# The last block of each MLP's down projection as seven quarter products

## The chip, the cores and the metric

The kernel runs on one core of one Trainium2 chip. The metric is the device time of one execution in microseconds. The kernel before takes 1024.99 us, the median of three runs (1024.59 to 1025.01). Five engines work side by side, each with its own queue: TensorE (PE in the profile; PEld are its weight loads), VectorE (DVE), ScalarE (ACT), GpSimd (POOL) and SyncE (SP), which issues most transfers. POOL issues the accumulating transfers, which add what they load to what stands in the tile.

## The reference

A trunk of two layers over 512 tokens of width 1024, all in float32. Each layer is a mixer, a layer norm, an MLP and a layer norm:

```python
def _layernorm(x, g, b):
    mu = xf.mean(-1, keepdims=True)
    var = jnp.square(xf - mu).mean(-1, keepdims=True)
    return ((xf - mu) * lax.rsqrt(var + LN_EPS) * g + b).astype(x.dtype)

def _mlp(x, w_up, w_down):          # w_up 1024 x 4096, w_down 4096 x 1024
    h = jax.nn.relu(x @ w_up)
    return (h * h) @ w_down

    for l in range(DEPTH):          # DEPTH = 2, alpha = sqrt(2)
        y = _mla(...) if l < n_a else _swa(...)
        x = _layernorm(alpha * x + y, ln_mix_g[l], ln_mix_b[l])
        x = _layernorm(alpha * x + _mlp(x, mlp_w_up[l], mlp_w_down[l]), ln_mlp_g[l], ln_mlp_b[l])
    return x
```

Layer 0 has latent attention (`_mla`), layer 1 sliding-window attention (`_swa`). The change touches the two calls of `_mlp` and the norm behind each.

## The kernel before

**Numbers in two parts.** Every matrix product takes its operands as a high part, rounded by ScalarE, and a low part, the rest, which is a subtraction on VectorE. `split` (L71 to L82) makes the two: ScalarE at L76, the low part at L79, on VectorE unless the caller names GpSimd. `three` (L107) turns one product into three matmuls: high by high, high by low, low by high.

**Blocks and sevens.** The hidden width of 4096 is cut into four blocks q of 1024. `up` of a block gives 1024 hidden values for 512 tokens, `down` multiplies them with the block's 1024 rows of `w_down` and adds to the residual stream `xs`, four row tiles of 128 tokens by 1024. Up of every block and down of blocks 0 to 2 are products of 2 x 2 quarters, made by a seven-product scheme. One quarter product of `down` covers 256 tokens (two row tiles t), 512 columns and a depth of 512 (four chunks m): 2 x 4 x 3 = 24 matmuls with 512 columns each. It takes a factor (a sum of hidden quarters, in the tile `fac`, three buffers) and a sum of weight quarters.

**Weights.** The sums of weight quarters are grown in place. `queue_seven` (L164) loads a quarter in two halves jp of 512 KB, splits it into `wh` and `wl` (four buffers each), and then lets POOL issue an accumulating transfer of the next quarter onto it (L188). So products 1, 5, 6 and 4 hang on one chain (tile `quada`), 3 and 7 on another (`quadb`), and 2 loads alone. Each link is a split, an accumulating transfer, and the next split. The function `weights` hands out the pairs in order and prepares at most four tiles ahead (`AHEAD`); a tile made "aside", in a spare place, doesn't count in that ring.

**Order.** PE and SP work strictly in the order of the program (`pe`, L92). On the other engines a planner orders what is ready by its own costs, with the order of the program as priority; `tc.high_priority()` puts a part ahead, and `pinned` keeps its vector instructions in order. The steps of an MLP are written out in `STEPS`, `FIRST_STEPS` and `LAST_STEPS` (L39, L40): U'5 is product 5 of up of block q + 1, D5 product 5 of down of block q. A factor is made two steps ahead of its product.

**The last block.** Down of block 3 is plain: `TokMajor` (L425) takes four row tiles, two halves of 512 columns and eight chunks, 192 matmuls, with eight plain weight tiles of 512 KB. Its `finish` (L451) first makes the left half of all row tiles, chunk pair by chunk pair, then the right half row tile by row tile. After each row tile come its add and statistics (`add_last`, L538; `count`, L520) and its norm (`layer_norm`, L387): aggregate, a root on POOL (`rsqrt_of`, L375), and two passes over the row tile on VectorE. In layer 0 the finished row tiles are turned for the next stage (`turn_tokens`, L404): eight transposes on PE, in its order, and a split. In layer 1 they go out.

**Before the last block**, the running sum `u2` of products 1 and 6 of blocks 0 to 2 is brought into `xs` by six vector instructions after D6 of block 2 (L778 to L782).

Of the kernel before, what the change touches and what calls it, by code (L numbers as in the profile page):

```python
# [15 lines left out]
P = 128  # L16
D = 1024
# [22 lines left out]
FIRST_STEPS, LAST_STEPS = "U'1 U'2 U'5 U'3 U'6 U'7 U'4 D'1 D'2", "U'1 D5 U'2 D3 U'5 D6 D7 U'3 U'6 U'7 U'4 D4"  # L40
# [8 lines left out]
def build(tc, nc, io, out):  # L49
    with ExitStack() as top:  # L50
# [113 lines left out]
        def queue_seven(name, key, chunk):  # L164
# [18 lines left out]
            def grown(a, jp, *more, aside=None):  # L183
                wh, wl = tiles_of_weights(aside)
                with behind(state.pop("first", None) if (key, a, jp) == ("U", "b", 1) else None):
                    split(wh, wl, flat(half(a, jp)), keep=(a, bool(more)) == ("b", True) and key == "U")
                if more:
                    nc.gpsimd.dma_start(half(a, jp), chunk(*more, jp), accum_op=ALU.add)  # L188
                return wh, wl
# [5 lines left out]
            def alone(jp, aside=None):  # L195
# [10 lines left out]
                4: lambda jp: grown("a", jp),  # L206
# [37 lines left out]
        def mlp_stream(l):  # L244
# [392 lines left out]
        def mlp(src, gb, dst, mp):  # L637
# [17 lines left out]
            class Block:  # L655
# [68 lines left out]
                def factor(self, n, quad=False):  # L724
                    if quad:
                        f = mp.tile([P, 2, 4, 256], F32R, tag="quada", bufs=1, name=nm("fac"))
                    else:
                        f = mp.tile([P, 2, 4, 256], F32R, tag="fac", bufs=3, name=nm("fac"))
                    g = [self.g.get(a) for a in ("a11", "a12", "a21", "a22")]
                    split(f[:, 0], f[:, 1], g[2] if n == 0 else self.down.sum(n, *g))  # L730
                    self.fac[n] = f

                def down_(self, n):
                    w = [weights("down") for _ in range(2)]
# [32 lines left out]
            for i, (which, q, n) in enumerate(steps):  # L767
                if which == "D":

                    i_q = steps.index(("U", q, {1: 6, 2: 2}.get(n, 4)))  # L770
                    i_last = steps.index(("U", q + 1, {2: 2, 3: 2}.get(n, 6))) - 1
                    at.setdefault(max(min(i - 2, i_last), i_q), []).append((q, n))
            for i, (which, q, n) in enumerate(steps):
                if which == "U":
                    blocks[q].up(n)
                else:
# [618 lines left out]
```

## Time and profile before

| | |
|---|---|
| time, median of 3 runs | 1024.99 us (1024.59 to 1025.01) |
| profiled execution: span | 1021.9 us; the page gives no time of its own beside it, and the median of the runs is 3.1 us above the span |
| mean granted TensorE clock | 0.992 |
| PE busy | 994.6 us, 97% of the span |
| DVE busy | 766.6 us, 75% |
| ACT busy | 555.9 us, 54% |
| POOL busy | 232.9 us, 23% |
| last block's 192 products in layer 1 | from 970.2 to 1014 us |
| last vector instruction | ends at 1018.7 us |

The times of a row of the profile are microseconds from the start of the span. In a row of the timeline come start, busy time, engine, line of the kernel, operation, tile written and tiles read, shape, how many instructions the row merges, and in brackets the idle time before them and what ended it. PE's rows overlap, since matmuls are pipelined; the cost of one is read from start to start. In a table by stretches each engine has its busy time and the number of its instructions; PEclk is the granted clock as a share of full speed.

### The profile page before, as it was taken

How to read it: one execution, taken by the hardware profiler on the slowest of the kernel's cores; microseconds unless marked ns; L12 is line 12 of the kernel's file. 1: busy time of each engine (PE TensorE's matmuls, PEld its weight loads, DVE VectorE, ACT ScalarE, POOL GpSimd, SP SyncE). 2: the span in 40 equal slices, each digit the busy share in tenths (PEclk: the TensorE clock that was granted, in tenths of full speed). 3: DMA queues.
4: the chain of work that ended last, by engine and by line, in shares of the span. 5: the costliest groups of instructions: out<-in, count | busy, mean ns of one | idle time of the engine just before them, and what ended most of it. 6: DMA issues, size and time to landing. Idle time of an engine off the chain costs nothing. (4 is left out here: it accounts for less than half of the span.)

```text
span 1021.9 us, 15865 instructions
## 1 busy us (share of the span) xinstructions
PE 994.6 (97%) x6148; PEld 895.9 (88%) x6148; DVE 766.6 (75%) x1227; ACT 555.9 (54%) x847; POOL 232.9 (23%) x204
## 2 busy tenths in 40 slices
PE   9999999989999999999999999999899999999996
PEld 8888887987999989998889898889799999998986
DVE  6588856888769858886585578688886896797756
ACT  5556643456637637646146688445654664665620
POOL 1232001312211211210014675223032122123002
PEclk9999999999999999999999999999999999999998
DMA  7421108389877976972332212349688798798332
GB/s 247 149 85 42 63 21 268 87 191 243 154 172 199 190 178 180 243 125 94 113 103 94 83 64 73 119 87 227 175 182 168 164 227 160 183 258 153 84 124 82
DMA packets 60247, 149.55 MB, mean 146 GB/s; under 512 B 5212, under 2 KB 9741, under 8 KB 60173
## 3 DMA queue, kind: packets, MB, share of 16 engines
q0 software_dynamic: 24320, 58.73, 32.1%
q1 hardware_dynamic: 35852, 89.82, 25.6%
q8 instruction: 48, 0.79, 0.3%
q14 instruction: 27, 0.21, 0.1%
HBM read 146.41 MB, written 4.22 MB: 147 GB/s over the span
## 5 line engine op out<-in xcount | busy, mean ns | idle before, releaser
L103 PE MATMUL mm<-wh,fac 128*128 128x512 f32 (+1 forms) x944 | 295.5, 390 | 4.6 <-ACT fac L76 3.0
L76 ACT ACTIVATE wh<-wq 128x1024 fp32r<-128x1024 f32 x164 | 173.5, 1060 | 202.5 <-PE mm L103 136.2
L79 DVE TENSOR_TENSOR wl<-wq,wh 128x1024 fp32r<-128x1024 f32 x164 | 199.7, 1221 | 80.4 <-ACT wh L76 79.3
L103 PE MATMUL mm<-xth,wh 128*128 128x256 f32 (+1 forms) x936 | 245.1, 290 | 5.3 <-DVE a L715 5.3
L103 PE MATMUL mm<-xth,wl 128*128 128x256 f32 (+1 forms) x808 | 234.7, 290 | 1.2 <-DVE wl L79 1.2
L103 PEld LDWEIGHTS mm<-wh,fac 128*128 128x128 f32 x944 | 177.6, 190 | 41.6 <-ACT fac L76 3.4
L103 PE MATMUL mm<-xtl,wh 128*128 128x256 f32 (+1 forms) x680 | 198.7, 292 | 0.0
L103 PE MATMUL mm<-wl,fac 128*128 128x512 f32 (+1 forms) x472 | 183.3, 388 | 0.0
L103 PEld LDWEIGHTS mm<-xth,wh 128*128 128x128 f32 x936 | 170.1, 192 | 8.5 <-issue 5.6
L103 PEld LDWEIGHTS mm<-xth,wl 128*128 128x128 f32 x808 | 154.7, 192 | 3.7 <-DVE wl L79 1.4
L188 POOL DMA_DIRECT2D wq<-in_up x64 | 77.5, 1218 | 277.1 <-DVE wl L79 209.7
L76 ACT ACTIVATE wh<-raw 128x1024 fp32r<-128x1024 f32 (+4 forms) x85 | 84.7, 998 | 98.1 <-PE mm L103 66.8
L103 PEld LDWEIGHTS mm<-xtl,wh 128*128 128x128 f32 x680 | 130.2, 191 | 3.0
L79 DVE TENSOR_TENSOR wl<-raw,wh 128x1024 fp32r<-128x1024 f32 (+3 forms) x64 | 75.6, 1189 | 38.9 <-ACT wh L76 38.8
L103 PEld LDWEIGHTS mm<-wl,fac 128*128 128x128 f32 x472 | 89.6, 190 | 17.1
L188 POOL DMA_DIRECT2D wq<-in_down x48 | 42.0, 875 | 188.1 <-DVE wl L79 168.9
L375 POOL TENSOR_TENSOR rs<-v,half 128x1 f32<-128x1 f32 x24 | 28.8, 1200 | 192.8 <-DVE v L394 156.5
L79 POOL TENSOR_TENSOR wl<-raw,wh 128x1024 fp32r<-128x1024 f32 (+2 forms) x21 | 43.8, 2090 | 79.5 <-ACT wh L76 77.0
L103 PE MATMUL mm<-wh,oh 128*128 128x512 f32 x128 | 50.9, 398 | 1.3 <-ACT wh L76 1.3
L103 PE MATMUL mm<-wl,oh 128*128 128x512 f32 x128 | 50.0, 390 | 0.8 <-DVE wl L79 0.8
L103 PE MATMUL mm<-wh,ol 128*128 128x512 f32 x128 | 50.0, 391 | 0.0
L532 DVE TENSOR_TENSOR x<-mm,x 128x512 f32<-128x512 f32 (+1 forms) x49 | 32.9, 675 | 13.9 <-PE mm L103 13.6
(218 smaller groups left out, 1845.1 us busy)
## 6 DMA issues: line engine op xcount, KB each, us to landing
wq<-in_up POOLq DMA_DIRECT2D x64, 512.0 KB, 7.6
wq<-in_down POOLq DMA_DIRECT2D x48, 512.0 KB, 6.5
wq<-in_up SPq DMA_DIRECT2D x32, 512.0 KB, 5.6
raw<-in_down SPq DMA_DIRECT2D x28, 512.0 KB, 6.8
wq<-in_down SPq DMA_DIRECT2D x24, 512.0 KB, 6.2
raw<-in_up SPq DMA_DIRECT2D x16, 512.0 KB, 4.0
raw<-in_w_o SPq DMA_DIRECT2D x8, 512.0 KB, 3.2
raw<-in_w_sq SPq DMA_DIRECT2D x8, 512.0 KB, 3.3
```

The costliest lines, as they stand in the source:

```text
L76: high = nc.scalar.activation(dst_h, src, AF.Copy)
L79: low = (engine or nc.vector).tensor_sub(dst_l, src, f32(dst_h))
L103: pe(nc.tensor.matmul(dst, st, mv, start=first and i == 0, stop=last and i == len(pairs) - 1, **kw))
L188: nc.gpsimd.dma_start(half(a, jp), chunk(*more, jp), accum_op=ALU.add)
L375: nc.gpsimd.tensor_tensor(r, v, half, ALU.pow)
L532: nc.vector.tensor_add(xs[t][:, c], b, xs[t][:, c])
```

## The change

Down of block 3 is taken in seven quarter products too, with the weights of a seventh `queue_seven`. `LAST_STEPS` becomes `STEPS` with five more steps: D4 of block 2 moves from behind U'4 to ahead of U'6, and after U'4 follow D'1, D'2, D'5, D'3, D'6, D'7 and D'4. The first five run as a product with both row tiles, as in the blocks before. D'6 makes row tiles 0 and 1 whole, so their norms come behind each of its two halves. D'7 and D'4 go together by row tile (`last_pair`): product 7 and product 4 of row tile 2, then those of row tile 3; in the last layer product 4 of row tile 3 is made in two halves of 256 columns.

For this block alone the low part of the second half of each grown weight tile is made on GpSimd, and product 4's weights go into two spare tiles of the pool `xt`. The six instructions that bring `u2` into `xs` move from VectorE after D6 of block 2 to GpSimd after D'1 (its own add on VectorE first). `TokMajor` and the plain weights are gone from the MLP. The factors need the sums of quarters that the sevens need; in the plain block they were the four quarters themselves.

```diff
-FIRST_STEPS, LAST_STEPS = "U'1 U'2 U'5 U'3 U'6 U'7 U'4 D'1 D'2", "U'1 D5 U'2 D3 U'5 D6 D7 U'3 U'6 U'7 U'4 D4"
+FIRST_STEPS, LAST_STEPS = "U'1 U'2 U'5 U'3 U'6 U'7 U'4 D'1 D'2", STEPS + " D'5 D'3 D'6 D'7 D'4"
...
             def grown(a, jp, *more, aside=None):
                 wh, wl = tiles_of_weights(aside)
+                low = nc.gpsimd if last and jp else nc.vector
...
-            add |= {("D", q): queue_seven("down", "D", down(q)) for q in range(NFF - 1)}
+            add |= {("D", q): queue_seven("down", "D", down(q), q == NFF - 1) for q in range(NFF)}
+
+            def spare_pair():
+                pair = xp.tile([P, 2, 1024], F32R, tag="xt", bufs=8, name=nm("w_xt"))
+                return pair[:, 0], pair[:, 1]
...
+                elif (which, q, n) == ("D", NFF - 1, 4):
+                    add[which, q](n, [spare_pair] * 2)
...
-            for c in range(8):
-                queue("down", io["down"][l, (NFF - 1) * 8 + c])
...
+                def products(self, n, f, w, t, b, cols=slice(0, 512), first=True):
+                    tk = slice(t * P, (t + 1) * P)
+                    for m in range(4):
+                        wh, wl = w[m // 2]
+                        c = slice(m % 2 * 512 + cols.start, m % 2 * 512 + cols.stop)
+                        group(
+                            b, three(f[:, 0, m, tk], f[:, 1, m, tk], wh[:, c], wl[:, c]),
+                            first and m == 0, m == 3, skip_group_check=True,
+                        )
+
+                def down_last(self, n):
+                    if n == 7:
+                        for t in range(2):
+                            self.last_pair(t)
+                        return
...
+                    for t in range(2):
+                        b = self.bank(("D", key), t)
+                        self.products(n, f, w, t, b, first=n not in (2, 3))
+                        if n == 1:
+                            nc.vector.tensor_add(u2[t], b, u2[t])
+                            nc.gpsimd.tensor_sub(xs[2 + t][:, highs], xs[2 + t][:, highs], u2[t])
+                            nc.gpsimd.tensor_sub(xs[t][:, highs], xs[t][:, highs], u2[t])
+                            nc.gpsimd.tensor_add(xs[2 + t][:, lows], xs[2 + t][:, lows], u2[t])
+                        elif n == 2:
+                            add_last(t, lows, b)
+                        elif n == 5:
+                            add_plain(2 + t, highs, b)
+                        elif n == 3:
+                            add_plain(t, highs, b)
+                        elif n == 6:
+                            whole(t, lambda: (take(t, highs, b), count(t, highs)))
+                            take(2 + t, highs, b)
+                            add_plain(2 + t, lows, b)
+
+                def last_pair(self, t):
+                    if t == 0:
+                        self.w74 = [[weights("down") for _ in range(2)] for _ in range(2)]
+                    b = bank()
+                    self.products(7, self.fac[7], self.w74[0], t, b)
+                    take(2 + t, highs, b)
+                    count(2 + t, highs)
+                    add_plain(2 + t, lows, b)
+                    n = 2 if dst is None and t == 1 else 1
+                    for i in range(n):
+                        c = slice(i * 512 // n, (i + 1) * 512 // n)
+                        b = bank(512 // n)
+                        self.products(4, self.fac[4], self.w74[1], t, b, c)
+                        if i < n - 1:
+                            add_last(2 + t, c, b)
+                    whole(2 + t, lambda: add_last(2 + t, c, b))
...
+            def whole(t, evac):
+                if not gbs:
+                    gbs.append(gb())
+                pinned[0] = dst is not None
+                with tc.high_priority():
+                    evac()
+                    layer_norm(t, gbs[0], dst)
+                if dst is not None and t == NT - 1:
+                    prepare(1)
+                pinned[0] = False
+                if dst is not None and t in (1, 2):
+                    with tc.high_priority():
+                        dst.turn(t - 1)
...
-                    if (q, n) == (NFF - 2, 6):
-                        for t in range(2):
-                            take(t, highs, u2[t])
-                            take(2 + t, highs, u2[t])
-                            add_plain(2 + t, lows, u2[t])
...
-            b = blocks[NFF - 1]
-            b.factor(2)
-            b.factor(1)
-            b.factor(4)
-            b.factor(0, True)
...
-            TokMajor(Hidden(), add_last, "down").finish(gb, dst, dst and (0, 0, 0, 1))
```

More of the change, by code (lines that the diff above doesn't have):

```diff
@@ L162, in build, with queue_seven @@
         mlp_pool = [None]
-        def queue_seven(name, key, chunk):
+        def queue_seven(name, key, chunk, last=False):
             quads = {}
@@ L184, in grown @@
                 wh, wl = tiles_of_weights(aside)
+                low = nc.gpsimd if last and jp else nc.vector
                 with behind(state.pop("first", None) if (key, a, jp) == ("U", "b", 1) else None):
-                    split(wh, wl, flat(half(a, jp)), keep=(a, bool(more)) == ("b", True) and key == "U")
+                    split(wh, wl, flat(half(a, jp)), low, keep=(a, bool(more)) == ("b", True) and key == "U")
                 if more:
@@ L721, in up_out, with factor @@
                         nc.scalar.activation(self.g[done], self.g[done], AF.Square)
[L724 to L728, printed above, removed]
+                def factor(self, n):
+                    f = mp.tile([P, 2, 4, 256], F32R, tag="fac", bufs=3, name=nm("fac"))
@@ L729, in factor @@
                     g = [self.g.get(a) for a in ("a11", "a12", "a21", "a22")]
-                    split(f[:, 0], f[:, 1], g[2] if n == 0 else self.down.sum(n, *g))
+                    split(f[:, 0], f[:, 1], self.down.sum(n, *g))
                     self.fac[n] = f
+                def products(self, n, f, w, t, b, cols=slice(0, 512), first=True):
[7 more added lines that the diff above has]
+                        )
@@ new lines, in down_last @@
+                def down_last(self, n):
[3 more added lines that the diff above has]
+                        return
+                    w = [weights("down") for _ in range(2)]
+                    f = self.fac.pop(n)
+                    key = {3: 5}.get(n) or own_bank[n]
+                    for t in range(2):
[16 more added lines that the diff above has]
+                            add_plain(2 + t, lows, b)
@@ L733, in down_ @@
                 def down_(self, n):
+                    if self.q == NFF - 1:
+                        self.down_last(n)
+                        return
                     w = [weights("down") for _ in range(2)]
@@ L773, in mlp @@
             for i, (which, q, n) in enumerate(steps):
+                if (which, q, n) == ("D", NFF - 1, 7) and dst is not None:
+                    state["hold"] = first_sq
                 if which == "U":
                     blocks[q].up(n)
-                else:
+                elif (q, n) != (NFF - 1, 4):
                     blocks[q].down_(n)
-                    if (q, n) == (NFF - 2, 6):
-                        for t in range(2):
-                            take(t, highs, u2[t])
-                            take(2 + t, highs, u2[t])
-                            add_plain(2 + t, lows, u2[t])
@@ L783, in mlp @@
                 for q_, n_ in sorted(at.get(i, ()), key=lambda x: [y[2] for y in steps if y[0] == "D" and y[1] == x[0]].index(x[1])):
                     blocks[q_].factor(n_)
-            b = blocks[NFF - 1]
-            b.factor(2)
-            b.factor(1)
-            b.factor(4)
-            b.factor(0, True)
-            class Hidden:
-                def h(self, k, cols):
-                    return self.of(0, k, cols)
-                def l(self, k, cols):
-                    return self.of(1, k, cols)
-                def of(self, p, k, cols):
-                    n = ((2, 1), (4, 0))[cols.start // 256][k // 4]
-                    return b.fac[n][:, p, k % 4, cols.start % 256 : cols.start % 256 + P]
@@ L803, in mlp @@
-            if dst is not None:
-                state["hold"] = first_sq
-            TokMajor(Hidden(), add_last, "down").finish(gb, dst, dst and (0, 0, 0, 1))
         ed = dr.tile([SQH, BANDW], F32, name="ed")
```

5 lines of the change are left out of this document (3 added, 2 removed).

## The prediction

> **What bounds the kernel now.** I read the page first, then the busy time by stretches, then the instructions of PE, DVE and POOL around the end of each MLP in order of time.
>
> ```profile
> span 1021.9 us, 15865 instructions
> PE 994.6 (97%) x6148; PEld 895.9 (88%) x6148; DVE 766.6 (75%) x1227; ACT 555.9 (54%) x847; POOL 232.9 (23%) x204
> ```
>
> TensorE sets the time. The shown runs' median of 1024.99 us lies 3.1 us above this span; I make the sum against the span and add the difference to the 3.1. By stretches (columns: span of time, its length, then busy PE, PEld, DVE, ACT, POOL, clock, DMA share, GB/s):
>
> ```profile
> 360.00:440.00 80.00, 80.00 (x512) 73.09 (x511) 61.68 (x65) 44.81 (x46) 16.69 (x16) 1.00 0.85 199
> 964.70:970.20 5.50, 5.50 (x26) 4.54 (x25) 4.65 (x6) 5.47 (x6) 0.00 (x0) 1.00 0.52 173
> 970.20:991.90 21.70, 21.70 (x97) 17.75 (x96) 10.59 (x12) 5.38 (x6) 0.00 (x0) 1.00 0.43 150
> 991.90:1013.70 21.80, 21.80 (x119) 18.95 (x118) 16.58 (x26) 1.06 (x1) 4.57 (x3) 1.00 0.12 48
> 1013.70:1021.90 8.20, 0.53 (x5) 0.33 (x3) 3.88 (x7) 0.00 (x0) 1.52 (x1) 0.69 0.33 128
> ```
>
> The middle of an MLP, already all in sevens, keeps PE at 80.00 of 80.00 with DMA at 0.85, so the sevens' transfers alone don't starve it. The last block (970.20 to 1013.70, second layer) is full on PE too, and DVE has room: 10.59 of 21.70, then 16.58 of 21.80. That room is what the change spends.
>
> **The change part by part.** *PE.* Three 512-column products take 0.68 us (start to start, first and third row):
>
> ```profile
> 400.08 0.61 PE L103 MATMUL mm<-wh,fac 128*128 128x512 f32 x2
> 400.54 0.39 PE L103 MATMUL mm<-wl,fac 128*128 128x512 f32 x1
> 400.76 0.61 PE L103 MATMUL mm<-wh,fac 128*128 128x512 f32 x2
> 964.60 0.40 PE L103 MATMUL mm<-wh,fac 128*128 128x512 f32 x1
> 514.54 1.03 PE L411 MATMUL tr<-ident,x 128*128 128x128 f32 x8
> 515.33 0.47 PE L103 MATMUL mm<-wh,fac 128*128 128x512 f32 x1
> 520.88 0.28 PE L103 MATMUL mm<-xth,wh 128*128 128x256 f32 x1
> 531.74 1.25 PE L411 MATMUL tr<-ident,x 128*128 128x128 f32 x8 [1.19 <-DVE xtl L79]
> ```
>
> One is 0.227 us. The plain block has 4 row tiles x 2 halves x 8 chunks x 3 = 192; seven quarter products have 7 x 2 x 4 x 3 = 168. So 24 x 0.227 = 5.4 us go per layer, 10.9 in all. A quarter product of 24 takes 5.4 us. I count from the end of U'4: D'1, D'2, D'5, D'3 end at 5.4, 10.9, 16.3, 21.8; D'6's row tiles at 24.5 and 27.2; the two pairs at 32.6 and 38.1. D4 (q = 2), which stood after U'4 (964.60), stands ahead of it; so old times are put on this count by taking off 964.60 + 5.44.
>
> *DVE.* Its prices, start to start:
>
> ```profile
> 967.53 1.22 DVE L79 TENSOR_TENSOR fac<-a,fac 128x1024 fp32r<-128x1024 f32 x1
> 968.67 0.68 DVE L532 TENSOR_TENSOR x<-mm,x 128x512 f32<-128x512 f32 x1
> 989.00 1.28 DVE L532 TENSOR_TENSOR x<-mm,x 128x512 f32<-128x512 f32 x2
> 990.19 1.28 DVE L526 BATCH_NORM_STATS2 bn<-x 128x6 f32<-128x512 f32 x2
> 991.39 1.51 DVE L532 TENSOR_TENSOR x<-mm,x 128x512 f32<-128x512 f32 x2
> 1009.98 0.21 DVE L391 BATCH_NORM_AGGREGATE mv<-bn 128x2 f32<-128x12 f32 x1
> 1010.22 0.15 DVE L394 TENSOR_SCALAR v<-mv 128x1 f32<-128x1 f32 x1
> 1010.29 1.28 DVE L396 SCALAR_TENSOR_TENSOR x<-x,mv,gb 128x1024 f32<-128x1024 f32 x1
> 1012.01 1.28 DVE L400 SCALAR_TENSOR_TENSOR x<-x,rs,gb 128x1024 f32<-128x1024 f32 x1
> 1014.27 0.42 DVE L532 TENSOR_TENSOR x<-mm,x 128x256 f32<-128x256 f32 x1 [0.64 <-PE mm L103]
> 1015.19 0.26 DVE L391 BATCH_NORM_AGGREGATE mv<-bn 128x2 f32<-128x24 f32 x1
> 1017.28 1.42 DVE L400 SCALAR_TENSOR_TENSOR x<-x,rs,gb 128x512 f32<-128x512 f32 x2 [0.44 <-POOL rs L375]
> ```
>
> A 1024-wide op is 1.14 us, a 512-wide add or count 0.60, a layer norm 0.24 + 0.07 + 1.2 + 1.2 = 2.7, and one half's add and count 0.9 (1014.27 to 1015.19), which I halve to 0.4 for a 256-wide count.
>
> Before, four row tiles end 5.4 us apart. Now two end inside D'6, 2.7 us apart, and each brings take, count, norm, take, add: 0.6 + 0.6 + 2.7 + 0.6 + 0.6 = 5.1. The first pair brings three ops, add, count and norm: 5.7. The second brings 0.6 + 0.8 + 0.6, two halves at 0.9 and the last norm, 3.5 (1015.19 to 1018.70): 7.3. With the low part of D'4's weights, 1.1, this is 10.2 + 5.7 + 7.3 + 1.1 = 24.3 us, and none of it but the last can start before D'6's first row tile at 24.5 (plus 0.2 until DVE sees it). DVE ends at 49.0 although PE ends at 38.1. Old: 1018.70 - 970.04 = 48.7. **So the last layer gains nothing: +0.3**, and any lateness s at D'6's first row tile is added in full. The 5.4 us of PE are hidden behind DVE.
>
> First layer: the next stage needs row tile 3 transposed, before at 531.74. Its last product ended at 520.88; less 216 x 0.227 and two transposes of 0.79 that is 470.3 for U'4's end, so 531.74 is 56.0 on my count. Now DVE needs 10.2 + 5.7 + 2.0, add, count and norm of row tile 3 (0.6 + 0.8 + 2.7, and 0.45 for POOL's root), four turns at 0.6, two w_k lows and D'4's: 28.2, from 24.7 to 52.9. That is -3.1, or -0.8 if row tile 2's turn and the w_sq low go ahead; I take -2.0. PE's transposes of row tile 0 stand, in its strict order, right behind D'6: they wait from 27.2 until the norm is done at 29.1 or later, with the pairs queued behind them; this stall is covered only because DVE is last.
>
> *POOL.* It takes the low parts of six second halves and six 512-wide updates of x after D'1, beside eight 512 KB accumulating DMAs.
>
> ```profile
> L79 POOL TENSOR_TENSOR wl<-raw,wh 128x1024 fp32r<-128x1024 f32 x13 | 31.1, 2399 | 45.8 <-ACT wh L76 45.8
> L188 POOL DMA_DIRECT2D wq<-in_down x48 | 42.0, 875 | 188.1 <-DVE wl L79 168.9 <-DMA wq<-in_up 12.9 <-DVE x L529 6.2
> wq<-in_down POOLq DMA_DIRECT2D x48, 512.0 KB, 6.5
> 644.62 1.30 POOL L79 TENSOR_TENSOR ol<-o,oh 128x512 fp32r<-128x512 f32 x1 [2.75 <-ACT oh L76]
> ```
>
> The updates start at 3.5 (D'1's first row tile at 2.7, DVE's add) and take 6 x 1.3 = 7.8. Queued behind them in POOL's order are a DMA issue (0.9) and D'5's low (2.4): ready at 14.6, while PE wants that half at 10.9 + 1.4 = 12.3. **s = 2.3** if POOL and DVE don't disturb each other. The next link, DMA 6.5, copy, low, keeps about that lateness at D'6.
>
> They do disturb each other, by these rows (POOL, DVE, DVE; then POOL's root over all 24, and one alone):
>
> ```profile
> 653.75 1.81 POOL L79 TENSOR_TENSOR ol<-o,oh 128x512 fp32r<-128x512 f32 x1 [7.83 <-ACT oh L76]
> 653.18 1.23 DVE L79 TENSOR_TENSOR wl<-raw,wh 128x1024 fp32r<-128x1024 f32 x1 [1.16 <-ACT wh L76]
> 654.65 1.99 DVE L79 TENSOR_TENSOR wl<-raw,wh 128x1024 fp32r<-128x1024 f32 x1 [0.25 <-ACT wh L76]
> L375 POOL TENSOR_TENSOR rs<-v,half x24: 549/1522/1532, 20.1 to 1015.7; 128x1 f32<-128x1 f32 x24
> 20.07 0.56 POOL L375 TENSOR_TENSOR rs<-v,half 128x1 f32<-128x1 f32 x1 [18.38 <-DVE sink L371]
> ```
>
> POOL's 1.30 us op, started inside a DVE op that reads two SBUF tensors, took 1.81 and ended 1.3 after that op; the next such DVE op took 1.99 in place of 1.23 and ended 1.1 after POOL. They ran one after the other. POOL's root takes 0.56 alone and 1.52 beside DVE's norm. In the present kernel such meetings are rare. In the new tail they are the rule: from 0 to 24.5 DVE has 14 two-tensor ops at 1.14 (five weight lows, five factor lows, four sums) = 16.0, and 6.6 of adds from PSUM and counts; POOL has 7.8 + 4 lows at 2.4 = 17.4. One after the other, 33.4 us don't fit in 24.5: s = 8.9 even if every PSUM add lies beside POOL; 6.5 if D'7's low slips past D'6's first tile; 10.3 if each of seven POOL ops in D'5's path waits out one DVE op (2.3 + 7 x 1.14). I take s = 8.5, near the sum. After D'6, POOL's last low and four roots (2.4 + 2.0) meet the norms: p from 0 to 4.4; I take 2.
>
> The Trainium skill, "SBUF — State Buffer", section "Who interferes with whom", says that a Vector instruction with two SBUF inputs contends with a GpSimd instruction that reads SBUF, and that the loser fully blocks. By that rule, which the rows above agree with, the moved lows save DVE nothing here, and the sum is that of "everything in turn" below; with no such rule it is that of "no collisions".
>
> Sum: +0.3 - 2.0 + 2 x (8.5 + 2) = **+19.3 us**, 1044.
>
> **The rivals.** *No collisions (port time free):* s = 2.3, p = 0, +2.9 us, 1028. For it: most POOL ops of the trace keep 2.40. Against: those lie beside DVE ops on PSUM.
>
> *Not slower:* the POOL queue puts weights ahead of the x updates, so s = 0, and DVE packs without a gap, D'4's low ahead of D'6: the last layer gives -0.8, the first -3.1, together -3.9, 1021; half-way 1023. It decides from s under 1 us. For it: PE without a stall in the middle stage; against: DVE at 22.6 of 24.5 before D'6, with nothing left for a wait.
>
> *Everything in turn, and the clock:* s = 10.3, p = 4.4: +27.7; a stall of several us also lowers PE's clock.
>
> ```profile
> 238.00:240.00 2.00, 1.29 (x3) 1.10 (x4) 2.00 (x3) 1.97 (x4) 0.00 (x0) 0.63 0.70 195
> 238.71 1.22 PE L103 MATMUL mm<-wh,fac 128*128 128x512 f32 x2 [0.82 <-DVE fac L79]
> 242.37 0.62 PE L103 MATMUL mm<-wh,fac 128*128 128x512 f32 x2
> ```
>
> From 238.71 to 242.37 nine products ran, 3.66 us in place of 2.04: 1.6 more, so +29.3, 1054.
>
> **How the numbers follow.** Forecast (1036 to 1050) 0.42; no collisions 0.20; all in turn 0.14; not slower 0.24, of which half is faster. About 0.2% (2 us) is what a measurement can tell from no change. Faster 0.12, same 0.12, slower 0.76. The range 1023 to 1056 leaves out the better half of "not slower" and what goes past "all in turn".
>
> **What would show it.** Right: DVE near full from U'4 to the end, POOL's 128x512 updates well over 1.3 us and lows over 2.4, DVE two-tensor ops over 1.3, PE waiting for POOL's wl in D'5 by 5 to 10 us, and DVE's last op more than 8 us behind PE's last product. Wrong: PE idle under 3 us per tail, POOL's updates at 1.3, or DVE ending under 6 us after PE.

## The result, and the profile after

The changed kernel takes **1064.52 us** (median of six runs, 1059.26 to 1065.83), the kernel before 1025.0 us on the same chip (six runs, 1023.84 to 1028.75). The ratio is 1.0358, with a 95% interval from 1.0334 to 1.0382; it is an estimate over all the runs of both, and the quotient of the two medians, 1.0386, lies just above it. Slower was forecast; 1044 was too low, and the time lies above the range's end of 1056.

The profiled execution is the quickest of the six (1059.26 us, 2.4 us above its span). Its page, first lines:

```profile
span 1056.9 us, 15878 instructions
PE 993.0 (94%) x6088; PEld 887.5 (84%) x6088; DVE 808.1 (76%) x1253; ACT 574.0 (54%) x865; POOL 305.8 (29%) x244
```

PE has 60 instructions fewer by the page, and the span is 35.0 us longer. The busy times by stretches (columns as in the prediction) follow the prediction's count: from the end of U'4 to the end of D'6's first row tile, from there to the transposes of row tile 0, on to those of row tile 3 (first layer); then the last layer, cut once.

```profile
477.07:510.90 33.83, 26.61 (x111) 19.75 (x110) 31.99 (x26) 17.51 (x18) 26.82 (x16) 1.00 0.62 145
510.90:526.86 15.96, 2.89 (x14) 2.05 (x12) 15.53 (x21) 5.07 (x5) 7.59 (x4) 0.71 0.47 99
526.86:551.19 24.33, 23.16 (x132) 20.64 (x132) 20.84 (x34) 7.38 (x13) 4.57 (x3) 0.91 0.19 65
992.38:1026.30 33.92, 26.74 (x111) 19.88 (x110) 32.10 (x26) 17.50 (x18) 26.95 (x16) 1.00 0.44 82
1026.30:1053.68 27.38, 16.37 (x73) 12.53 (x71) 25.44 (x42) 3.18 (x3) 12.09 (x7) 0.87 0.36 96
```

D'6's first row tile ends 33.8 us (first layer) and 33.9 us (last) after U'4, where PE alone needs 24.5: s is 9.3 and 9.4. VectorE, 10.59 of 21.70 and 16.58 of 21.80 in the old last block, is now, in the same layer, at 32.10 of 33.92 ahead of that point and at 25.44 of 27.38 behind it. The first layer's tail is 33.83 + 15.96 + 24.33 = 74.1 us against 56.4, **+17.7** (in the old kernel D4's first product starts at 469.92; the prediction had worked out 470.3, and so 56.0). The last layer's is 33.92 + 27.38 = 61.3 against 48.7, **+12.6**. PE's waits, in order of time, the first layer's and then two of the last:

```profile
471.25 0.48 PE L103 MATMUL mm<-xth,wh 128*128 128x256 f32 x2 [2.04 <-DVE a L721]
491.46 0.50 PE L103 MATMUL mm<-wl,fac 128*128 128x512 f32 x1 [0.81 <-POOL wl L79]
498.10 0.50 PE L103 MATMUL mm<-wh,fac 128*128 128x512 f32 x1 [2.45 <-ACT fac L76]
502.24 0.50 PE L103 MATMUL mm<-wl,fac 128*128 128x512 f32 x1 [1.46 <-POOL wl L79]
509.60 0.50 PE L103 MATMUL mm<-wl,fac 128*128 128x512 f32 x1 [1.62 <-POOL wl L79]
526.86 1.97 PE L417 MATMUL tr<-ident,x 128*128 128x128 f32 x8 [13.07 <-DVE v L400]
...
986.55 0.47 PE L103 MATMUL mm<-xth,wh 128*128 128x256 f32 x2 [2.06 <-DVE a L721]
1036.86 2.50 PE L103 MATMUL mm<-w_xt,fac 128*128 128x512 f32 x5 [1.94 <-POOL w_xt L79]
```

Two of these were not in the sum. PE stands 13.07 us ahead of row tile 0's transposes, where 1.9 had been allowed. And it stands 2.04 and 2.06 us ahead of U'4, at whose end the prediction's count starts. 17.7 + 12.6 + 2.0 + 2.1 = 34.4 of the 35.0 us. Another 5.3 us lie between the profiled execution and the median; the other five runs have spans of 1059.1 to 1063.4 us at mean clocks of 0.971 to 0.979 (the profiled one: 0.984), and no profile of this kernel shows where. Executions differ ahead of the change too: PE's first product with a factor in the first layer starts at 236.7 us in this profile, at 237.2 in that of the kernel before, and between 235.8 and 240.2 in those of the experiments.

The collisions are there, first in POOL's rows of the last layer (start, duration):

```profile
998.88 2.26 POOL L762 TENSOR_TENSOR x<-x,u 128x512 f32<-128x512 f32 x1
1001.11 2.27 POOL L763 TENSOR_TENSOR x<-x,u 128x512 f32<-128x512 f32 x1
1003.35 3.36 POOL L79 TENSOR_TENSOR wl<-wq,wh 128x1024 fp32r<-128x1024 f32 x1
```

and then in VectorE's:

```profile
1002.15 2.31 DVE L79 TENSOR_TENSOR fac<-uv,fac 128x1024 fp32r<-128x1024 f32 x1
1004.39 0.68 DVE L538 TENSOR_TENSOR x<-mm,x 128x512 f32<-128x512 f32 x1
1004.99 2.80 DVE L591 TENSOR_TENSOR uv<-uv,a 128x1024 f32<-128x1024 f32 x1
1015.12 3.45 DVE L79 TENSOR_TENSOR fac<-uv,fac 128x1024 fp32r<-128x1024 f32 x1
```

The six updates per layer take 2.2 to 2.3 us where 1.30 was the price alone. Three of the lows per layer take 3.0 to 3.4 where it was 2.40. Of VectorE's sums and factors five per layer take 2.2 to 3.45 for 1.14, while an add from PSUM keeps its 0.68. The chain of work that ended last goes through them, in the last layer (seven of its rows: start, duration, what):

```profile
970.06 12.73 DMA wq<-in_up
1001.11 2.27 POOL x L763
1003.38 3.33 POOL wl L79
1011.13 2.27 POOL x L763
1013.91 7.30 DMA wq<-in_down
1025.35 7.94 DMA wq<-in_down
1034.45 2.36 POOL w_xt L79
```

The x updates hold up the low parts, these the next accumulating transfer, that the next low part, down to D'4's weights (w_xt). The first row is a transfer of U'4's weights: it lands at 982.8, and behind it come its split and the VectorE operation that releases PE's wait of 2.06. Last, VectorE's work between D'6's first row tile (510.9) and the end of row tile 0's norm in the first layer (L79 are low parts, L659 takes, L532 counts, L397 a norm's aggregate, L406 its second pass):

```profile
511.15 1.21 DVE L79 TENSOR_TENSOR wl<-wq,wh 128x1024 fp32r<-128x1024 f32 x1
512.28 1.21 DVE L79 TENSOR_TENSOR fac<-a,fac 128x1024 fp32r<-128x1024 f32 x1
513.42 1.27 DVE L659 TENSOR_TENSOR x<-x,mm 128x512 f32<-128x512 f32 x2
...
515.21 0.68 DVE L532 BATCH_NORM_STATS2 bn<-x 128x6 f32<-128x512 f32 x1
515.98 1.23 DVE L79 TENSOR_TENSOR w_xt<-wq,w_xt 128x1024 fp32r<-128x1024 f32 x1
...
518.91 3.08 DVE L79 TENSOR_TENSOR wl<-raw,wh 128x1024 fp32r<-128x1024 f32 x1
521.92 0.20 DVE L397 BATCH_NORM_AGGREGATE mv<-bn 128x2 f32<-128x12 f32 x1
...
525.52 1.28 DVE L406 SCALAR_TENSOR_TENSOR x<-x,rs,gb 128x1024 f32<-128x1024 f32 x1 [0.34 <-POOL rs L381]
```

VectorE does not stop; it does other things. Row tile 0's count is done at 515.9, its aggregate starts at 521.92, and the norm ends at 526.8, 15.9 us after the row tile's last product and not 4.6.

### The profile page after: what moved, and what is told of

Same layout as the page of the kernel before. It is cut to its first block, busy times and chain, and to the rows that moved or that the text cites. A ratio compares the mean times of both kernels' runs of the same rounds, so it can differ in the third digit from the quotient of the medians.

```text
span 1056.9 us, 15878 instructions
## 1 busy us (share of the span) xinstructions
PE 993.0 (94%) x6088; PEld 887.5 (84%) x6088; DVE 808.1 (76%) x1253; ACT 574.0 (54%) x865; POOL 305.8 (29%) x244
## 5 line engine op out<-in xcount | busy, mean ns | idle before, releaser
L76 ACT ACTIVATE wh<-wq 128x1024 fp32r<-128x1024 f32 x184 | 194.2, 1060 | 233.2 <-PE mm L103 148.3
L79 DVE TENSOR_TENSOR wl<-wq,wh 128x1024 fp32r<-128x1024 f32 x174 | 213.9, 1233 | 98.6 <-ACT wh L76 97.6
L103 PE MATMUL mm<-wh,fac 128*128 128x512 f32 x864 | 277.8, 396 | 11.3 <-ACT fac L76 7.9
L103 PEld LDWEIGHTS mm<-wh,fac 128*128 128x128 f32 x864 | 164.3, 191 | 49.0 <-ACT fac L76 9.1
L103 PEld LDWEIGHTS mm<-xth,wh 128*128 128x128 f32 x936 | 170.1, 192 | 12.6 <-issue 9.8
L103 PE MATMUL mm<-wl,fac 128*128 128x512 f32 x432 | 171.1, 396 | 8.2 <-POOL wl L79 8.2
L189 POOL DMA_DIRECT2D wq<-in_down x64 | 57.4, 932 | 221.2 <-DVE wl L79 217.8
L103 PEld LDWEIGHTS mm<-wl,fac 128*128 128x128 f32 x432 | 82.4, 191 | 27.2 <-POOL wl L79 11.2
L76 ACT ACTIVATE wh<-raw 128x1024 fp32r<-128x1024 f32 (+4 forms) x73 | 72.0, 987 | 60.1 <-PE mm L103 34.0
L79 DVE TENSOR_TENSOR wl<-raw,wh 128x1024 fp32r<-128x1024 f32 (+3 forms) x52 | 62.8, 1217 | 17.0 <-ACT wh L76 16.9
L79 POOL TENSOR_TENSOR wl<-raw,wh 128x1024 fp32r<-128x1024 f32 (+2 forms) x21 | 43.7, 2088 | 79.7 <-ACT wh L76 79.7
L79 DVE TENSOR_TENSOR fac<-uv,fac 128x1024 fp32r<-128x1024 f32 x32 | 48.1, 1510 | 3.5 <-ACT fac L76 3.5
```

The lines of the kernel that those rows point to most:

```text
L76: high = nc.scalar.activation(dst_h, src, AF.Copy)
L79: low = (engine or nc.vector).tensor_sub(dst_l, src, f32(dst_h))
L103: pe(nc.tensor.matmul(dst, st, mv, start=first and i == 0, stop=last and i == len(pairs) - 1, **kw))
```

## The experiments

A tail is the time from the first product of D'1 (or where it could have begun, where it waits for a factor) to PE's transposes of row tile 3 (first layer) or to the end of VectorE's last operation (last layer). Ratios are against the kernel before on the same chip, with 95% intervals; the changed kernel has 1.0358 [1.0334, 1.0382]. A tail and a wait are read from one execution. In the five experiments that leave the changed kernel's last layer as it is and alter only the first layer's end, the last tail is 61.4 to 63.3 against 61.3, so a difference of 2 us between two tails shows little by itself.

| run | median us | ratio | first tail | last tail | PE's wait for row tile 0 |
|---|---|---|---|---|---|
| before | 1025.0 | 1 | 56.4 | 48.7 | none |
| changed | 1064.52 | 1.0358 | 74.1 | 61.3 | 13.07 |
| last layer only | 1039.54 | 1.0151 [1.0114, 1.0189] | 56.3 | 60.9 | none |
| first layer only | 1045.96 | 1.0220 [1.0192, 1.0249] | 74.6 | 48.6 | 13.16 |
| transposes later | 1061.57 | 1.0344 [1.0323, 1.0365] | 70.7 | 63.3 | 6.37 |
| x updates on VectorE | 1058.30 | 1.0311 [1.0285, 1.0336] | 72.3 | 60.4 | 14.95 |
| lows on VectorE | 1069.82 | 1.0411 [1.0384, 1.0439] | 78.8 | 65.7 | 13.07 |
| loads later | 1069.80 | 1.0423 [1.0401, 1.0445] | 79.7 | 66.9 | 12.10 |
| GpSimd's work left out | 1049.63 | 1.0246 [1.0209, 1.0283] | 68.8 | 56.7 | 11.54 |
| norm's second pass left out | 1056.67 | 1.0321 [1.0291, 1.0351] | 72.2 | 59.2 | 11.36 |
| next stage's lows left out | 1059.84 | 1.0344 [1.0316, 1.0373] | 71.5 | 62.7 | 12.30 |
| norm first | 1062.28 | 1.0358 [1.0332, 1.0384] | 75.1 | 61.9 | 9.35 |
| all of VectorE's and GpSimd's relief | 1031.09 | 1.0057 [1.0038, 1.0077] | 55.8 | 51.5 | 0.44 |

**Each layer alone.** The steps, the stream of weights and the old end of the MLP are chosen by layer:

```diff
-            for i, (which, q, n) in enumerate(steps_of()):
+            for i, (which, q, n) in enumerate(steps_of(l == NEW_LAYER)):
...
+            if l != NEW_LAYER:
+                for c in range(8):
+                    queue("down", io["down"][l, (NFF - 1) * 8 + c])
```

> The change in the last layer alone; the first layer's MLP ends as before the change. Theory (the two tails cost different amounts, since only in the first layer PE stands 13 us for row tile 0's norm): the last layer keeps its +12.7 us of tail and some 2 us of wait ahead of U'4, so +13 to +17 us over the kernel before, 1038 to 1042, and PE has no idle of over 4 us at the end of the first layer. Rival (both layers cost the same, as the prediction had it but for 2 us): about half of the +39.5, +18 to +22 us, 1043 to 1047.

> The change in the first layer alone; the last layer ends as before the change. Theory (the layers' costs add, and the last layer alone cost +13.0 us): +21 to +27 us over the kernel before, 1046 to 1053, with the 13 us wait for row tile 0's norm in it. Rival (the costs don't add, part of what both together lose comes from elsewhere, as from the clock): +18 us or less, or +30 or more.

The ratios multiply to 1.0374, within the interval of both together: the layers' losses add, +1.5% and +2.2%. The prediction had the first layer as the cheaper one; it is the dearer.

**GpSimd's six updates on VectorE, from PSUM.**

```diff
-                            nc.vector.tensor_add(u2[t], b, u2[t])
-                            nc.gpsimd.tensor_sub(xs[2 + t][:, highs], xs[2 + t][:, highs], u2[t])
-                            nc.gpsimd.tensor_sub(xs[t][:, highs], xs[t][:, highs], u2[t])
-                            nc.gpsimd.tensor_add(xs[2 + t][:, lows], xs[2 + t][:, lows], u2[t])
+                            take(2 + t, highs, b)
+                            take(t, highs, b)
+                            add_plain(2 + t, lows, b)
```

(and u2 is taken into x after the last block but one, as before the change)

> The changed kernel with the x updates moved: the running sum u2 goes into x after D6 of block 2 as before the change (six VectorE instructions), and D'1's product goes into x by three VectorE instructions per row tile straight from PSUM; the six GpSimd instructions of 2.2 to 2.3 us are gone. Nothing is left out. Theory (the port): VectorE has 4 instructions of 0.6 us more in the tail, but they read one SBUF tensor and GpSimd's 13.5 us of updates no longer stand in turn with VectorE's two-tensor instructions nor ahead of D'5's low part: D'6's first row tile ends 5 to 8 us earlier in each layer, 10 to 16 us faster in all than the changed kernel. Rival (VectorE's own amount alone bounds): 2.4 us per layer more on VectorE, 0 to 5 us slower.

The ratio falls by 0.0047, 4.8 us: the sign is the theory's, the size less than half of it. The low parts stay on GpSimd and still meet VectorE, so its two-tensor operations go on taking up to 4 us.

**The low parts back on VectorE.**

```diff
-                low = nc.gpsimd if last and jp else nc.vector
+                low = nc.vector
```

> The changed kernel with the low parts of all the last block's weights on VectorE, none on GpSimd. Nothing is left out. Theory (the port): a low part on GpSimd takes 2.4 us of the shared access, one on VectorE 1.14; six per layer move, so 0 to 4 us per layer faster than the changed kernel. Rival (GpSimd's work is free for VectorE): 6 x 1.14 = 6.8 us per layer more on the engine that bounds, 8 to 14 us slower.

The rival's sign: 0.0053 more, 5.4 us. VectorE has no room for them: put back they cost more than they did on GpSimd, so the collisions do not make the two places equal. PE waits up to 8.09 us for factors, whose sums VectorE makes later.

**GpSimd's work left out.**

```diff
-                            nc.gpsimd.tensor_sub(xs[2 + t][:, highs], xs[2 + t][:, highs], u2[t])
...
+                    if last and jp:
+                        nc.scalar.activation(wh, flat(half(a, jp)), AF.Copy)
+                        nc.scalar.activation(wl, flat(half(a, jp)), AF.Copy)
```

> GpSimd's new work is gone: the six updates of x after D'1 are left out (x lacks u2), and the low parts of the last block's second weight halves are left out (ScalarE writes a plain copy in their place). Theory (what GpSimd's port time costs VectorE, and the lateness of its lows, is most of what D'6 is late by, s = 9.3 to 9.5 us per layer): VectorE's two-tensor operations fall back to 1.14 us, D'6's first row tile ends 6 to 9 us earlier in both layers, the kernel takes 1042 to 1050 us, 15 to 22 us less than the changed kernel. Rival (the tails are set by VectorE's amount of work behind D'6 and by PE's waits; the collisions lie in their shadow): under 8 us less, 1057 or more.

Both tails of this run by stretches, in the same columns (POOL is the fifth busy time: issues and roots alone):

```profile
478.29:547.09 68.80, 52.39 (x253) 43.80 (x252) 58.31 (x78) 35.34 (x42) 12.41 (x10) 0.90 0.48 116
988.01:1044.74 56.73, 41.23 (x181) 32.96 (x180) 49.04 (x67) 26.08 (x27) 11.27 (x10) 0.92 0.44 95
```

D'6's first row tile comes 3.3 us earlier in the first layer and 3.6 in the last (30.5 and 30.4 us after U'4; s falls from 9.3 and 9.4 to 6.0 and 5.9), not the 6 to 9 of the theory. The tails are 5.3 and 4.6 us shorter, and the ratio falls by 0.0112, 11.5 us, a size between the two expectations. GpSimd's part is some 10 of the 35 us, not all of the loss; with only the roots left to meet VectorE, the kernel is still 1.0246 of the kernel before, where the prediction's sum without collisions gave +2.9 us. Some of what is left is the run's own. ScalarE carries 12 more copies, two of them ahead of D'1's factor in each layer; PE waits 1.29 and 1.32 us for that factor in the first layer (1.31 and 1.31 in the last) and comes back at a clock of 0.53 and 0.54 for over 3 us. So the 10 us are rather too low than too high. But from D'6's first row tile on, the first layer still takes 38.3 us (40.3 in the changed kernel), where the prediction had 28.2.

**The loads of the last block later.** The second and third group of D' loads were tied to U'7's first result:

```diff
+            def late(ap):
+                if last:
+                    nc.vector.tensor_copy(ap, state["late"])
...
+                if a == "b":
+                    late(half(a, jp)[:, 0, 0:1])
...
+                late(raw[:, 0:1])
```

> The changed kernel with four of the six early 512 KB loads of the last block (product 2's and product 3's weights) held back until the first evacuation of U'7, by a one-column write that they must wait for. Nothing is left out. Theory (these loads at 964.5 to 967.3 delay the two accumulating transfers of U'4's weights, which landed after 11.5 and 12.7 us instead of 7.4, and so PE by 2.04 and 2.06 us ahead of U'4): those two stalls vanish, 3 to 4 us faster than the changed kernel. Rival (the stall is the planner's order on VectorE): no change, the stalls stay.

The wait ahead of U'4 is gone in both layers, so these loads do make it. The ratio grows all the same, by 0.0065: PE now waits for the late weights behind U'4, up to 2.57 us at a time, and further on up to 4.15 us for VectorE's adds. The issues of the transfers that U'4 waits for show what it is about, between 960 and 985 us after the change (line, engine, count, size, median us from issue to landing):

```profile
wq<-in_down SPq DMA_DIRECT2D x4, 512.0 KB, 10.1
wq<-in_up POOLq DMA_DIRECT2D x3, 512.0 KB, 11.5
raw<-in_down SPq DMA_DIRECT2D x2, 512.0 KB, 6.9
```

and before it, between 938 and 955 us:

```profile
wq<-in_up POOLq DMA_DIRECT2D x4, 512.0 KB, 6.5
```

Six loads of 512 KB go out together from 964.52 on, in the midst of the accumulating ones, and these land after 11.5 us and not 6.5.

**Row tile 0's transposes later.** They go behind the first pair of products, row tile 1's behind the first half of the second pair:

```diff
-                if dst is not None and t in (1, 2):
+                if dst is not None and t == 2:
                     with tc.high_priority():
-                        dst.turn(t - 1)
+                        dst.turn(0)
...
+                    if dst is not None and t == 1:
+                        with tc.high_priority():
+                            dst.turn(1)
```

> The changed kernel with one edit in the first layer: row tile 0 is turned behind the first pair of products 7 and 4, row tile 1 behind product 7 of the second pair, instead of right behind D'6 and the first pair. Nothing is left out. Theory (PE's strict order exposes the norm of row tile 0: the 13.07 us idle of PE ahead of the transposes at 526.86 is real loss, since the pairs and then VectorE's work on them start that much later): about 9 us faster than the changed kernel, with no idle of more than 3 us on PE there. Rival (VectorE is last anyway, as my prediction had it, and the stall is covered): within 2 us of the changed kernel, the wait turning up at row tile 1, 2 or 3 instead.

The wait is halved, the tail is 3.4 us shorter, and the ratio is not told apart from the changed kernel's. A second edit was to let w_k's preparation in later, alone and together with this one; it missed its aim. In the trace w_k's two low parts stand where they were, and w_sq's and w_v's first weights come in a pair earlier:

```diff
-                    state["hold"] = first_sq
...
+                    if dst is not None and t == 1:
+                        state["hold"] = first_sq
+                        prepare(0)
```

> The preparation of w_k (two loads, two low parts of weights on VectorE) is let in one pair of products later, so that it no longer stands between row tile 0's count and its norm. Theory (VectorE's amount of work sets the first layer's tail, PE's wait is only partly exposed, by VectorE's 3.9 us of idle behind it): the wait of 13.07 us ahead of row tile 0's transposes becomes 8 to 10 us, and the time falls by 1 to 4 us, to 1060 to 1064. Rival (PE's wait sets the tail by itself): the time falls by as much as the wait, 3 to 5 us or more; or (w_k wanted at once by the next stage) the time doesn't fall at all.

> Both: w_k's preparation let in one pair later, and the transposes of row tile 0 put behind the first pair of products, those of row tile 1 behind the second pair's first product. Theory (VectorE's work sets the tail): PE's wait for row tile 0's norm falls from 13.07 us to under 4, and the time by no more than 3 to 6 us, 1058 to 1062. Rival (PE's wait is what makes the first layer's tail cost 18 us rather than 8.5): the time falls by 9 to 13 us, 1051 to 1055.

Alone: 1062.90 us, ratio 1.0373 [1.0341, 1.0406], a wait of 13.57, no gain. Together: 1058.37 us, 1.0341 [1.0293, 1.0389], a first tail of 71.7. There PE's waits read:

```profile
520.80 5.06 PE L103 MATMUL mm<-w_xt,fac 128*128 128x512 f32 x11 [2.58 <-DVE w_xt L79]
530.83 1.97 PE L417 MATMUL tr<-ident,x 128*128 128x128 f32 x8 [4.97 <-DVE v L400]
542.19 0.39 PE L103 MATMUL mm<-xtl,wh 128*128 128x256 f32 x1 [2.32 <-DVE xtl L79]
```

The 13 us are cut up, and 9.9 us of them come back as three waits, each for VectorE.

> Three mends in one: the six updates of x are made by VectorE from PSUM, u2 taken in ahead as before the change; w_k is prepared a pair later; the transposes of row tiles 0 and 1 stand a pair later. Theory (VectorE's work is the bound, so the mends that only move work give little each): 1051 to 1057 us, the sum of the single gains (5 by the first, 2 to 6 by the other two), still 25 us or more behind the kernel before. Rival (the mends unlock each other, since PE's waits went from one place to the next): 1045 or less.

With the x updates on VectorE as well: 1056.43 us, ratio 1.0309 [1.0282, 1.0336], tails of 69.5 and 59.8. By the ratio that is what the x updates gave alone; the mends don't unlock each other.

**VectorE's work left out.** The norm's second pass of row tiles 0 to 2 in both layers:

```diff
-                pin(nc.vector.scalar_tensor_tensor(x[:, c], x[:, c], r, gb[:, 1, c], ALU.mult, ALU.add))
+                if not skip:
+                    pin(nc.vector.scalar_tensor_tensor(x[:, c], x[:, c], r, gb[:, 1, c], ALU.mult, ALU.add))
```

> In the norms at the end of both MLPs the second pass (by rs and the bias) is left out for row tiles 0 to 2: VectorE has three 128x1024 operations of 1.2 us less per tail, and three waits for GpSimd's root. Theory (VectorE's amount of work sets both tails): each tail is 3.6 us shorter, to 4.5 with the waits for the root, 7 to 9 us together, 1055 to 1058. Rival (VectorE is not what binds the first layer, PE's waits and products are): the last layer gives 3.6 or more, the first under 1.5, or, by way of an earlier row tile 0, over 6.

and the low parts of the next stage's first weights:

```diff
-            queue("w_k", io["w_k"][m])
+            queue("w_k", io["w_k"][m], None)
...
+                    if low is None:
+                        pin(nc.scalar.activation(wl[:, c], raw[:, c], AF.Copy))
```

> The low parts of the next stage's first weights (two of w_k, the first of w_sq, two of w_v) are left out: ScalarE writes a plain copy in their place, so VectorE has four operations of 1.14 us less in the first layer's tail, one of which took 3.08 us beside GpSimd. The last layer is as in the changed kernel. Theory (VectorE's work sets the first layer's tail, and these four, of which the prediction had counted two, are in it): 4 to 7 us less, 1057 to 1061, with PE's wait for row tile 0's norm at 9 to 11 us. Rival (PE's wait and half clock set that tail): the time falls by less than 2 us, or exactly by what the wait falls by.

Three passes (3.6 us) gave back 1.9 and 2.1 us of the tails: VectorE's busy time in them falls by 3.5 and 3.7 us, and its idle time grows by 1.5 and 1.7. Four lows, 6.6 us in the changed kernel's trace, gave 2.6 in the first; VectorE's busy time falls by only 3.8 us there, and its idle time grows by 1.2. Both theories were too sharp. These gains are little more than two executions differ by, and the intervals of both ratios overlap the changed kernel's, so neither run shows by itself that VectorE's work sets the tails.

**Norm first.** Only VectorE's order is changed: nothing may come between row tile 0's count and its norm (beside the lines shown, the takes and adds are held in the program's order).

```diff
+                if dst is not None and t == 0:
+                    prepare(2)
...
-                if (which, q, n) == ("D", NFF - 1, 7) and dst is not None:
-                    state["hold"] = first_sq
+                if (which, q, n) == ("D", NFF - 1, 6) and dst is not None:
+                    state["hold"] = first_sq - 4
```

> VectorE's order alone is changed at the end of the first layer: row tile 0's aggregate and norm come right behind its count; the low parts of D'4's and of w_k's weights and the takes of row tile 2 come behind that norm (the low parts of D'4's and w_k's weights are let in only then). No instruction is added or left out, and the last layer is as in the changed kernel. Theory (PE's in-order chain sets the first layer's tail: 24.3 us of full PE work follow the wait, so the wait is exposed in full, and it is long because 11 us of other VectorE work stand between row tile 0's last product and its norm): PE's wait of 13.07 us falls to 5 to 8, the first layer's tail from 74.1 to 67 to 71, the time by 3 to 7 us, to 1057 to 1061. Rival (VectorE's amount of work is the bound as well, so the wait only moves to the pairs or to the next row tile): the wait falls as much, but the tail stays within 2 us of 74.1 and the time at 1062 or more.

PE's two waits in this run:

```profile
525.77 1.97 PE L417 MATMUL tr<-ident,x 128*128 128x128 f32 x8 [9.35 <-DVE x L406]
537.82 1.26 PE L417 MATMUL tr<-ident,x 128*128 128x128 f32 x8 [2.69 <-DVE x L406]
```

and on VectorE the operation ahead of row tile 0's take, then the second norm pass:

```profile
514.96 3.40 DVE L79 TENSOR_TENSOR fac<-a,fac 128x1024 fp32r<-128x1024 f32 x1
522.35 3.36 DVE L406 SCALAR_TENSOR_TENSOR x<-x,rs,gb 128x1024 f32<-128x1024 f32 x1
```

The rival's case. The two waits are 9.35 + 2.69 = 12.0 us in place of 13.07, the tail 75.1, the ratio the same to the fourth place. Two operations of 1.2 us took 3.4 each, behind a low part on GpSimd. VectorE is busy for 38.89 of the 41.17 us behind D'6's first row tile, by stretches:

```profile
513.60:554.77 41.17, 28.39 (x145) 24.16 (x143) 38.89 (x53) 12.57 (x18) 11.72 (x7) 0.83 0.29 76
```

> The same order, and the six updates of x on VectorE from PSUM, u2 taken in ahead, as before the change. Theory (the order in the first layer and GpSimd's updates in both are separate losses): the gain of the order (3 to 7 us) and that of the updates (4.8 us by the ratios of that experiment) add, 1052 to 1057; still 27 us or more behind the kernel before. Rival (one hides the other): 1057 to 1060, no better than the updates alone (1058.3).

With the x updates on VectorE: 1059.11 us, 1.0340 [1.0314, 1.0365], a first tail of 74.0 and a last one of 58.4. The gains don't add; the rival's 1057 to 1060 holds.

**All of the relief at once.** Norms of row tiles 0 to 2 left out, GpSimd's work left out, the next stage's lows left out, by the edits above.

> VectorE and GpSimd are relieved in both tails: the norms of row tiles 0 to 2 are left out (both passes), the six updates of x after D'1 are left out, the low parts of the last block's second weight halves and of the next stage's first weights are left out (ScalarE writes plain copies). PE's products are those of the changed kernel. Theory (PE's saving is real, and VectorE's and GpSimd's work hides it and more): PE's wait for row tile 0 falls under 5 us, the first layer's tail from 74.1 under 60, the last layer's from 61.3 under 52, the time to 1022 to 1036. Rival (something else holds the tails, as PE's clock, the late weights or ScalarE): a tail of over 64 in the first layer or over 55 in the last, 1040 or more.

The two tails of this run by stretches, same columns:

```profile
476.53:532.28 55.75, 49.71 (x252) 40.96 (x252) 46.60 (x68) 38.40 (x45) 8.36 (x10) 1.00 0.60 148
972.64:1024.18 51.54, 41.27 (x180) 33.07 (x180) 42.78 (x61) 26.07 (x27) 8.35 (x10) 0.97 0.49 105
```

The tails fall by 18.3 and 9.8 us, the ratio by 0.0301, 31 us; PE is then busy for 49.71 of 55.75 at a clock of 1.00. What VectorE and GpSimd do in the tails is most of the loss. Even so nothing of PE's 10.9 us shows: 1.0057 of the kernel before, which had none of its work left out. ScalarE's copies delay D'1's factor in this run too: PE waits 1.29 and 1.31 us for it in each layer, 5.2 us in all, about what is left of the loss. No run leaves the same norms and lows out of the kernel before, so what they would give there is open; its VectorE had room to spare in the last layer (10.59 of 21.70 us, then 16.58 of 21.80). No run beat the kernel before.

## Why the prediction was right, and where it was wrong

**The direction and most of the mechanism were right.** PE's saving of 5.4 us per layer is hidden, as the last layer said ("the last layer gains nothing"). Where VectorE's and GpSimd's two-tensor operations meet, they run one after the other: updates at 2.27 for 1.30, lows at up to 3.4 for 2.40, VectorE's two-tensor operations at up to 3.45 for 1.14. The Trainium skill, "SBUF — State Buffer", section "Who interferes with whom", says of such a pair that whoever issues first decides which one blocks; the trace agrees, with updates stretched behind VectorE's operations (2.27) and factors behind GpSimd's lows (3.45). s, taken as 8.5 from bounds of 6.5 and 10.3, measured 9.3 and 9.4. But collisions are only part of s, which is still 6.0 and 5.9 with GpSimd's work left out, 3 us or more of it that run's own. And the prediction's "the moved lows save DVE nothing here" was wrong: moved back to VectorE, they cost 5.4 us.

**The last layer was about right.** Forecast 0.3 + 8.5 + 2 = 10.8; measured 12.6, of which s is 0.9 more and the rest, p, 27.4 - 24.5 = 2.9 against 2 (24.5 is the 24.3 and the 0.2 until VectorE sees the product). That p came out near is in part luck: it was to be GpSimd's low and roots beside the norms, and in the chain there is also PE at half clock. Behind its wait of 1.94 us for D'4's weights the clock is 0.50 from 1036.86 to 1040.00, five products take 2.30 us in place of 1.13, and VectorE is idle for 0.84 us until the add behind them. VectorE's last operation ends at 1053.7, 8.4 us behind the end of PE's last product (24 products from 1042.28 for 3.03 us): as foretold.

**The first layer's sum failed**: "Now DVE needs 10.2 + 5.7 + 2.0, add, count and norm of row tile 3 ..., four turns at 0.6, two w_k lows and D'4's: 28.2, from 24.7 to 52.9". From D'6's first row tile to row tile 3's transposes it took 40.3 us (15.96 + 24.33), busy for 36.4 and idle for 3.9. Beside what was counted there are in that stretch, by its rows: the low part of D'7's weights, the last factor and an add, which the sum had ahead of D'6's first row tile (2.9); w_k's first low at 3.08, 1.9 above its price; the lows of w_sq and w_v (2.3); two turns more, the second cut off by the end of the stretch (0.7); three operations of the next stage (1.2). That is 9.0, and the idle time 3.9, of which 0.45 was counted. Together they make up the 12.1 that were missing, and 0.3 more by which the rest of the work stayed under its price. So the tail took 74.1 and not 64.5 (56.0 + 8.5); the 9.6 between them are, within 0.2, the 12.1 less the 2 of p, less the 1.1 by which the forecast had already gone from -3.1 to -2.0, and 0.8 in s.

**"This stall is covered only because DVE is last."** The stall was taken as 1.9 us, from 27.2 to 29.1; it is 13.07: the sum put the norm straight behind the row tile's last product, take and count, and VectorE's order had 11 us of other work from that product to the norm's end. Whether it is covered has two answers. PE, once released, is busy for 23.16 of 24.33 us up to the end of the tail, so from there on PE is the chain. But making the wait shorter (6.37, 4.97) or moving the norm forward (9.35) changed the time by nothing that can be told, because VectorE, busy for over 90% of the tail, came up next. So the wait is VectorE's load as it shows on PE, and not a second loss beside it.

**"The sevens' transfers alone don't starve it."** The middle stage is not this stage: six loads ahead of D', issued together, meet U's last accumulating transfers. Priced at nothing, this costs 2.0 and 2.1 us in the profiled execution, and the run with later loads, in which both waits are gone, shows that the loads are the cause.

**The rivals.** "No collisions" (+2.9) was too cheap: with GpSimd's work left out the loss was still 2.5%. Without collisions the prediction had only s = 2.3 a layer beside +0.3 and -2.0, and so none of the work that it had not counted behind D'6's first row tile. "Everything in turn, and the clock" (1054) named the half clock, for one stall: after the 13 us PE ran at 0.50, by the stretch behind that wait in the changed kernel.

```profile
527.00:530.00 3.00, 3.00 (x12) 2.71 (x13) 2.55 (x3) 1.19 (x2) 1.47 (x1) 0.50 0.02 5
```

The eight transposes took 1.62 us (526.86 to 528.48) in place of 0.79, and eight products from 528.48 to 531.74 took 3.26 in place of 1.82, 2.3 us more in all. The last layer has it too, behind the wait of 1.94 us above: seven products took 3.14 in place of 1.59. Of the signs, "PE waiting for POOL's wl in D'5 by 5 to 10 us" was wrong in its place: D'5 waits 0.81, and much of the lateness is spread over D'3's factor (2.45), the halves of D'3 and D'6 (1.46 and 1.62).

In the working itself one reading was slightly off, beside the 56.0: the GpSimd operation at 653.75 ended 1.15 us behind VectorE's and not 1.3, which changes no term.

**Still open.** How the last 5.3 us between the profiled execution and the median come about; how much of the loss GpSimd's part is beyond 10 us; and how the two chains of the first layer share the loss, since each single mend was eaten by the other and only the joint relief showed the whole.

## What to carry to other kernels

Fewer products on the bounding engine help only as far as the engine behind it can take its results sooner; count that engine's work over the whole stretch, with what other work has been pushed into it and with the next stage's preparations, not only the operations that the change names. A wait of the bounding engine for a nearly full one is a sign of the full one's load: moving the wait, or the operation waited for, moves the loss elsewhere. When operations of two engines run in turn, moving work from the one to the other frees less than the work's own time: here the loss with GpSimd's part left out was 11.5 us smaller, and with six lows per layer (6.8 us of VectorE's time each layer) put back on VectorE only 5.4 us larger in all.

## What was not expected of the hardware

A VectorE operation of 1.14 us that meets a 128x1024 low part on GpSimd can take three times as long: the factors, norm passes and weight lows quoted above took 3.08 to 3.45 us. Accumulating transfers of 512 KB, 6.5 us in the median before, took 11.5 when six plain loads of that size were under way. After a wait of 13 us PE came back at half clock for some 4 us (0.50 from 527 to 530), which cost 2.3 us. After a wait of only 1.94 us, with one of 0.17 just ahead of it, the clock was 0.50 for 3.1 us too (1036.86 to 1040.00), while after waits of 2.04 and 2.45 us it was 1.00 (471 to 473 and 498 to 501): the length of one wait doesn't decide it.
